# One in four low parts of the weights made by an accumulating DMA instead of a subtraction on VectorE

## The chip, the cores and the metric

The kernel runs on one core of one Trainium2 chip. The metric is device time in microseconds (us) for one call of the whole block. A core has a matrix engine (TensorE, PE in the profile), VectorE (DVE), ScalarE (ACT), GpSimd (POOL) and SyncE (SP), each with an instruction queue of its own, and 16 DMA engines that all queues share.

## The reference

One block of a language model on 256 tokens of width 2048 (T = 256, D = 2048), in float32: a gated feed-forward layer with half its output added, a mixer of an mLSTM and an HGRN2 recurrence behind one wide projection, a cross attention to a memory of 256 rows, and a second feed-forward layer, each behind a root-mean-square norm.

```python
def swiglu(h, w1, w3, w2):
    return (jax.nn.silu(h @ w1) * (h @ w3)) @ w2
...
        h = rmsnorm(x, norm_ffn1[l])
        x = x + 0.5 * swiglu(h, ffn1_w1[l], ffn1_w3[l], ffn1_w2[l])
        h = rmsnorm(x, norm_mix[l])
        (mq, mk, mv, mo, mi, mf, hq, hf, hi, hg, gate_m, gate_h) = jnp.split(h @ w_in[l], split_points, axis=-1)
...
        merged = jax.nn.sigmoid(gate_m) * (y_m @ w_proj_m[l]) + jax.nn.sigmoid(gate_h) * (y_h @ w_proj_h[l])
        x = x + merged @ w_out[l]
        h = rmsnorm(x, norm_xattn[l])
        m = rmsnorm(mem, norm_mem[l])
        x = x + cross_attention(h, m, xattn_wq[l], xattn_wkv[l], xattn_wo[l])
        h = rmsnorm(x, norm_ffn2[l])
        x = x + 0.5 * swiglu(h, ffn2_w1[l], ffn2_w3[l], ffn2_w2[l])
    return rmsnorm(x, norm_final)
```

D_FF is 5632, and w_in has 11272 columns. Nearly all the arithmetic is in products of 256 rows of activations with weights that are each used once.

## The kernel before

**Products in three terms.** TensorE multiplies in the type F32R, which keeps fewer bits than float32. So each operand is held as two tiles: `hi`, the value rounded to F32R, and `lo`, what is left, value minus `hi`. A product is the sum of three matmuls: high by high, high by low, low by high. In `gemm_nat`, whose output has tokens on the partitions, these are lines L200 (activation high, weight `hi`), L201 (activation high, weight `lo`) and L202 (activation low, weight `hi`), in this order, with 512 columns of weight streaming through (344 in three products of the mixer). In `gemm_tr`, whose output is transposed, they are L235, L236 and L237; the weight is the stationary operand there, and `lo` comes third.

**Units and subunits.** The weights of a product are cut into units, of 4 row blocks of 128 by 512 columns in `gemm_nat` and of 8 row blocks by 256 columns in `gemm_tr`: 1 MB each. A unit is loaded by one DMA from SyncE's queue (`load`, L148) into a buffer `wr`, of which there are 4. A unit has two subunits. Each is split by itself into tiles `wh` and `wl` of 128 partitions by 1024 elements, of which there are 4 buffers each: a cast on ScalarE (L159) rounds to `hi`, and a subtraction on VectorE (L160) makes `lo`. The 12 matmuls of a subunit in `gemm_nat`, or 24 of half the columns in `gemm_tr`, then use both.

**The order of the work.** The kernel first writes down a list of steps: subunits, and functions in between (evacuations of a finished product, and work that is put into a background list). `run` walks through the list. Before the matmuls of a subunit are issued, the units of the next 7 subunits are loaded and the next 3 subunits are split; after them `tick` issues what is due by then: transposes of new activations, norms, or one piece of the recurrences. The order in which instructions are issued is the order in each engine's queue. A tile framework adds the waits between engines, so that a cast waits until TensorE has read the last subunit out of the `wh` buffer that it fills, and a load waits until both subunits of the unit in its `wr` buffer are split. These lines set how far ahead all this goes:

```python
    SPLIT_AHEAD = 3
    LOAD_AHEAD = 7
        self.wraw = pool("wraw", 4)
        self.whi = pool("whi", 4)
        self.wlo = pool("wlo", 4)
```

ScalarE also evacuates products (L466 the silu of the feed-forward layers) and rounds activations that were turned (L292, L297, L263); VectorE turns activations in blocks of 32 by 32 (L286), makes their low parts (L293, L298, L264) and adds to the residual (L449, L451). GpSimd does 15 small powers for the norms (`rstd_of`, L407) and two memsets in the mixer; it issues no DMA. ScalarE's queue issues a few DMAs of constants and gains.

Of the kernel before, what the change touches and what calls it, by code (L numbers as in the profile page):

```python
# [12 lines left out]
F32 = mybir.dt.float32  # L13
F32R = mybir.dt.float32r
AF = mybir.ActivationFunctionType
ALU = mybir.AluOpType
# [3 lines left out]
P = 128  # L20
T = 256
# [40 lines left out]
class Sub:  # L62
    def __init__(self, unit, index, mm):
        self.unit, self.index, self.mm = unit, index, mm
        self.hi = self.lo = None
# [8 lines left out]
class Block:  # L74
# [3 lines left out]
    def __init__(self, ctx, tc, a, out):  # L78
        self.tc, self.nc, self.a, self.out = tc, tc.nc, a, out
        pool = lambda name, bufs, **kw: ctx.enter_context(tc.tile_pool(name=name, bufs=bufs, **kw))  # L80
        self.const = pool("const", 1)
        self.xp = pool("xp", 1)
# [3 lines that stand above are left out]
        self.s4 = pool("s4", 22)  # L86
        self.s2 = pool("s2", 4)
        self.small = pool("small", 4)
        self.acc = pool("acc", 4, space=PSUM)
        self.tr = pool("tr", 4, space=PSUM)  # L90
        self.steps = []
        self.now = 0
        self.timed = []
        self.bg = deque()
        self.uid = 0

    def nm(self, s):
        self.uid += 1
        return f"{s}_{self.uid}"
# [14 lines left out]
    def pacc(self, shape, name="pa"):  # L114
        return self.acc.tile(shape, F32, name=self.nm(name), tag="acc")

    # ---- the order of work
    def do(self, fn):
        self.steps.append(fn)

# [29 lines left out]
    def split(self, s):  # L150
        if s.hi is not None:
            return
        u = s.unit
        self.load(u)
        nk = u.nk // u.nsub
        raw = u.raw[:, s.index * nk:(s.index + 1) * nk, :]
        s.hi = self.whi.tile([P, nk, u.n], F32R, name=self.nm("wh"), tag="wh")
        s.lo = self.wlo.tile([P, nk, u.n], F32R, name=self.nm("wl"), tag="wl")
        self.nc.scalar.copy(s.hi, raw)  # L159
        self.nc.vector.tensor_sub(s.lo, raw, s.hi.bitcast(F32))  # L160

    def run(self):
        subs = [s for s in self.steps if isinstance(s, Sub)]
# [11 lines left out]
            i += 1  # L175
        self.flush()

    # ---- products; an operand is a list of (hi, lo) tiles of four 128-row pieces each
    def gemm_nat(self, ops, wap, n0, n, evac, kts=None, row0=0, late=0):
        """late: in the last subunits of the weights the second token tile waits until the first is done."""  # L180
        nc = self.nc
        box = {}
        pairs = ops
        nkt = 4 * len(pairs) if kts is None else kts

        def mm_for(k0, nk):
            def mm(hi, lo, ts=(0, 1)):
                if k0 == 0:
                    box["ps"] = [self.pacc([P, n]) for _ in range(2)]
                if k0 >= nkt - 2 * late and len(ts) == 2:  # L190
                    ts = (0,)
                    box.setdefault("late", []).append(lambda: mm(hi, lo, (1,)))
                for j in range(nk):
                    kt = k0 + j
                    xh, xl = pairs[kt // 4]
                    for t in ts:
                        sl = slice(t * P, (t + 1) * P)
                        a_h, a_l = xh[:, kt % 4, sl], xl[:, kt % 4, sl]
                        o = box["ps"][t]
                        nc.tensor.matmul(o, a_h, hi[:, j, :], start=(kt == 0), stop=False)  # L200
                        nc.tensor.matmul(o, a_h, lo[:, j, :], start=False, stop=False)  # L201
                        nc.tensor.matmul(o, a_l, hi[:, j, :], start=False, stop=(kt == nkt - 1))  # L202
            return mm

        for k0 in range(0, nkt, 4):
            u = Unit(wap, row0 + k0 * P, 4, n0, n, 2)
            for q in range(2):
                self.steps.append(Sub(u, q, mm_for(k0 + 2 * q, 2)))
        if not late:
            self.do(lambda: evac(box["ps"]))  # L210
            return

        def finish():
            evac(box["ps"], (0,))
            for f in box["late"]:
                f()
            evac(box["ps"], (1,))
        self.do(finish)
# [25 lines left out]
        self.do(lambda: evac(box["ps"]))  # L244

    def turn(self, src, gain, dst, halves=(0, 1)):
        """dst: (hi, lo) of the transposed 512 columns that src(t) gives, each times its gain."""
        nc = self.nc
        hi, lo = dst
        for h in halves:  # L250
            ps = self.ps([P, 2, T])
            for j in range(2):
                for t in range(2):
                    c = (2 * h + j) * P
                    nc.tensor.transpose(ps[:, j, t * P:(t + 1) * P], src(t)[:, c:c + P], self.ident)  # L255
            if gain is None:
                nc.scalar.copy(hi[:, 2 * h:2 * h + 2, :], ps)
                nc.vector.tensor_sub(lo[:, 2 * h:2 * h + 2, :], ps, hi[:, 2 * h:2 * h + 2, :].bitcast(F32))
            else:
                for j in range(2):  # L260
                    k = 2 * h + j
                    g = gain[:, k:k + 1]
                    nc.scalar.activation(hi[:, k, :], ps[:, j, :], AF.Copy, scale=g)  # L263
                    nc.vector.scalar_tensor_tensor(  # L264
                        lo[:, k, :], in0=ps[:, j, :], scalar=g, in1=hi[:, k, :].bitcast(F32),
                        op0=ALU.mult, op1=ALU.subtract)
# [6 lines left out]
        self.after(ticks + 1, lambda: self.turn(src, gain, dst, (1,)))  # L273

    def turn_on_vector(self, src, gain, dst, ticks=1):
        """The same for a tile of two token tiles, in blocks of 32 x 32 and without the tensor engine."""
        nc = self.nc
        box = {}
        sv = src.rearrange("p t (k j c) -> p t k j c", k=4, j=4)

        def blocks(i):
            if i == 0:
                box["t"] = self.t4([P, 4, T], name="tt")
            dv = box["t"].rearrange("p k (t i c) -> p t k i c", t=2, i=4)
            for j in range(4):
                nc.vector.transpose(dv[32 * j:32 * j + 32, :, :, i, :], sv[32 * i:32 * i + 32, :, :, j, :])  # L286

        def parts():
            hi, lo = dst
            tt = box["t"]  # L290
            if gain is None:
                nc.scalar.copy(hi, tt)  # L292
                nc.vector.tensor_sub(lo, tt, hi.bitcast(F32))  # L293
                return
            for k in range(4):
                g = gain[:, k:k + 1]
                nc.scalar.activation(hi[:, k, :], tt[:, k, :], AF.Copy, scale=g)  # L297
                nc.vector.scalar_tensor_tensor(lo[:, k, :], in0=tt[:, k, :], scalar=g, in1=hi[:, k, :].bitcast(F32),  # L298
                                               op0=ALU.mult, op1=ALU.subtract)

        for i in range(4):
            self.after(ticks + i, lambda i=i: blocks(i))
        self.after(ticks + 4, parts)

    # ---- pieces
    def setup(self):
        nc, a = self.nc, self.a
        c = self.const.tile([P, C_END], F32, name="cst")
# [177 lines left out]
                self.gemm_nat(LazyOps(lambda us=us: us, f1 - f0), w2, c * 512, 512, evac, row0=f0 * 512,  # L486
                              late=4 if end and last and c == 3 else 0)

    # ---- the two mixers
    def row_scale(self, n):  # L490
        nc = self.nc
        d = self.t2([P, 2, P], name="dg")
# [7 lines left out]
    def mixer(self, norm, chunk_done):  # L500
        nc, a = self.nc, self.a
# [8 lines left out]
        first = [True]  # L510
# [4 lines left out]
                first[0] = False  # L515
            nc.vector.tensor_mul(dst, ps, self.R)

        # forget gates and queries of HGRN2, two heads at a time
        for g in range(4):
            b, hh = g // 2, 2 * (g % 2)  # L520

# [29 lines left out]
            self.gemm_nat(ops, w, 6152 + 512 * j, 512, nat_evac(HB, "g", j, AF.Silu))  # L551
        self.do(lambda: [self.bg.extend(self.hgrn_out(H[b], HB, b)) for b in range(2)])

        # output gate of the mLSTM with its input and forget gates
        MO = [None] * 2

        def evac_o(j):
# [42 lines left out]
            self.gemm_nat(ops, w, 1024 + 512 * j, 512, nat_evac(MV, "v", j))  # L600
        self.do(lambda: self.bg.extend(self.mlstm_out(M, MV, MO)))

        # gates of the merge, projections
        merged = [None] * 4
        G = {}
        for c in range(4):
# [30 lines left out]
            self.gemm_nat(LazyOps(lambda: merged, 4), a["w_out"][0], 512 * c, 512, evac)  # L637

    def hgrn_levels(self, h, b):
        """A^T of four heads. A pair s < t meets at one scale l: both lie in one block of 4 l, in different  # L640
        pieces of l. The decay from s to the end of its piece goes to k, the rest of the decay to q."""
        nc = self.nc
        S = {}
        flat = lambda t: t.rearrange("p h t -> p (h t)")
# [141 lines left out]
        nc.scalar.activation(dst, dst, AF.Silu, bias=self.col["mlstm_conv_b"][:, ch:ch + 1])  # L786

    def mlstm_weights(self, m):
        """exp(log weight - m_t) of every pair and m_t itself, per head, time t on the partitions."""
        nc = self.nc  # L790
        gs = m["gates"]
        m["mt"] = self.small.tile([P, 4, 2], F32, name="mt", tag="mt", bufs=1)
# [42 lines left out]
    def mlstm_scores(self, m):  # L835
# [39 lines left out]
        for h in range(4):  # L875
            ths += [lambda h=h: head(h), lambda h=h: turn(h)]
# [34 lines left out]
            ths += [lambda b=b: turn(b)]  # L911
        return ths

    # ---- cross attention
    def mem_prep(self):
        nc = self.nc
        mem, self.memT = [None] * 4, [None] * 4
# [136 lines left out]
                self.add_to_x(c, ps, 1.0, lambda: chunk_done(c))  # L1054
            self.gemm_nat(LazyOps(lambda: O, 4), wo, 512 * c, 512, evac)

    # ---- all of it
    def build(self):
        nc, a = self.nc, self.a
        N = {}  # L1060
# [24 lines left out]
        def done(name):  # L1085
            return lambda c: self.norm_chunk(begin(name), c)
# [21 lines left out]
        turn_gains = self.setup()  # L1108
        self.ffn(lambda: N["norm_ffn1"], a["ffn1_w1"][0], a["ffn1_w3"][0], a["ffn1_w2"][0], done("norm_mix"))
        self.mixer(lambda: N["norm_mix"], done("norm_xattn"))  # L1110
        # the memory is normalised while the merge is projected
        self.insert_mem()
        self.cross_attention(lambda: N["norm_xattn"], done("norm_ffn2"))

# [6 lines left out]
        n = len(self.steps)  # L1121
# [43 lines left out]
```

## Time and profile before

| | us |
|---|---|
| median of 2 runs | 2570.2 (2569.82 to 2570.57) |
| span of the profiled execution | 2567.6 |
| TensorE busy | 2543.7 |
| VectorE busy | 1649.9 |
| ScalarE busy | 1187.4 |
| GpSimd busy | 14.3 |
| TensorE clock granted, mean | 0.998 |

For the profiled execution only the span from its first to its last instruction is shown, not a time of its own as the runs have; the median stands 2.6 us above that span. The profile comes from this one execution. Busy time counts the time in which an engine has an instruction in work; matmuls are pipelined, so a matmul that is listed with 0.39 us starts 0.23 us after the one before it. HBM reads come to 475.94 MB, 186 GB/s over the span. In an instruction group, the line of the kernel comes first, then engine, operation, what is written and read, the number of instructions, busy time and the mean of one, and the idle time of the engine before them with what ended it.

### The profile page before, as it was taken

The page shows a single profiled execution, that of the slowest core. Times are in us where ns is not written, and L with a number is a line of the kernel's source. Part 1 is how long each engine was busy: PE and PEld are TensorE (multiplying, and loading weights), DVE is VectorE, ACT ScalarE, POOL GpSimd, SP SyncE. Part 2 cuts the span into 40 slices and gives each one's busy share as a digit, 9 for nine tenths or more (in the row PEclk, how much of TensorE's full clock was granted, in tenths as well). Part 3 has the DMA queues.
Part 4 walks back from the last instruction along what each step waited for, and adds up shares of the span by engine and source line. Part 5 has one row for each costly group of instructions (what it writes and reads, how often), then busy time and mean ns, then how long its engine had stood idle before and what let it go on. Part 6 is the DMA issues. An engine that isn't in the chain of part 4 may idle for free.

```text
span 2567.6 us, 31614 instructions
## 1 busy us (share of the span) xinstructions
PE 2543.7 (99%) x12779; PEld 2176.6 (85%) x12779; DVE 1649.9 (64%) x2211; ACT 1187.4 (46%) x1385; POOL 14.3 (1%) x21
## 2 busy tenths in 40 slices
PE   8999999999999999999999999999999999999998
PEld 7888888888899899878888898998888888888887
DVE  5666644757768768576667844556757574456664
ACT  5444434444446555454445544454544443344443
POOL 0000000000000000000000000000000000000000
PEclk9999999999999999999999999999999999999999
DMA  7555555555554435545556555544555555555653
GB/s 266 190 197 197 193 190 192 196 197 187 197 189 166 158 123 191 175 163 193 197 194 215 181 181 197 183 146 158 188 195 195 197 185 197 193 197 186 215 191 130
DMA packets 271987, 480.09 MB, mean 187 GB/s; under 512 B 8008, under 2 KB 71776, under 8 KB 271840
## 3 DMA queue, kind: packets, MB, share of 16 engines
q1 hardware_dynamic: 270688, 476.15, 55.0%
q8 instruction: 100, 1.64, 0.3%
q10 hardware_dynamic: 1152, 1.92, 0.2%
q14 instruction: 47, 0.39, 0.0%
HBM read 475.94 MB, written 2.10 MB: 186 GB/s over the span
## 4 chain that ended last, share of the span: by engine, by line
PE 96%; DVE 2%; issue 1%; DMA 0%; ACT 0%; POOL 0%; SPq 0%; ACTq 0%; POOLq 0%
PE pa L201 27%; PE pa L202 27%; PE pa L200 27%; PE pa L236 4%; PE pa L237 4%; PE pa L235 4%; DVE tt L286 1%; PE ps L718 1%; DVE wl L160 1%; PE ps L255 0%; DMA x<-in_x 0%; PE ps L982 0%; PE ps L981 0%; PE ps L980 0%; POOL rstd L407 0%
## 5 line engine op out<-in xcount | busy, mean ns | idle before, releaser
L160 DVE TENSOR_TENSOR wl<-wr,wh 128x1024 fp32r<-128x1024 f32 (+1 forms) x904 | 1095.6, 1214 | 828.4 <-ACT wh L159 823.0
L159 ACT CAST wh<-wr 128x1024 fp32r<-128x1024 f32 (+1 forms) x904 | 942.2, 1044 | 1163.7 <-PE pa L202 1012.3
L200 PE MATMUL pa<-wh,oh 128*128 128x512 f32 (+1 forms) x3168 | 1233.6, 389 | 2.5 <-ACT wh L159 2.5
L201 PE MATMUL pa<-wl,oh 128*128 128x512 f32 (+1 forms) x3168 | 1228.8, 388 | 6.5 <-DVE wl L160 6.5
L202 PE MATMUL pa<-wh,ol 128*128 128x512 f32 (+1 forms) x3168 | 1228.0, 388 | 0.0
L201 PEld LDWEIGHTS pa<-wl,oh 128*128 128x128 f32 x3168 | 596.2, 188 | 126.8 <-DVE wl L160 8.1
L200 PEld LDWEIGHTS pa<-wh,oh 128*128 128x128 f32 x3168 | 596.0, 188 | 121.6 <-ACT wh L159 2.9
L202 PEld LDWEIGHTS pa<-wh,ol 128*128 128x128 f32 x3168 | 595.9, 188 | 120.3
L235 PE MATMUL pa<-oh,wh 128*128 128x256 f32 x896 | 254.9, 285 | 0.0
L236 PE MATMUL pa<-ol,wh 128*128 128x256 f32 x896 | 253.6, 283 | 0.0
L237 PE MATMUL pa<-oh,wl 128*128 128x256 f32 x896 | 253.6, 283 | 0.0
L236 PEld LDWEIGHTS pa<-ol,wh 128*128 128x128 f32 x896 | 172.0, 192 | 0.1
L235 PEld LDWEIGHTS pa<-oh,wh 128*128 128x128 f32 x896 | 172.0, 192 | 0.1
L237 PEld LDWEIGHTS pa<-oh,wl 128*128 128x128 f32 x896 | 171.9, 192 | 0.0
L286 DVE STREAM_TRANSPOSE tt<-sil 32x256 f32<-32x256 f32 x352 | 153.6, 436 | 6.8
L286 DVE STREAM_TRANSPOSE tt<-x 32x256 f32<-32x256 f32 x144 | 62.8, 436 | 2.7
L297 ACT ACTIVATE oh<-tt,cols 128x256 fp32r<-128x256 f32 x52 | 23.0, 500 | 48.1 <-DVE tt L286 48.1
L292 ACT CAST oh<-tt 128x1024 fp32r<-128x1024 f32 x25 | 26.4, 1055 | 33.2 <-DVE tt L286 33.2
L466 ACT ACTIVATE sil<-pa,rstd 128x512 f32<-128x512 f32 x44 | 29.8, 690 | 18.1 <-PE pa L202 18.0
L263 ACT ACTIVATE oh<-ps,cols 128x256 fp32r<-128x256 f32 x44 | 20.6, 473 | 27.7 <-DVE ol L264 22.8
L471 DVE SCALAR_TENSOR_TENSOR sil<-pa,rstd,sil 128x512 f32<-128x512 f32 x44 | 31.0, 743 | 0.0
L293 DVE TENSOR_TENSOR ol<-tt,oh 128x1024 fp32r<-128x1024 f32 x25 | 30.5, 1219 | 0.2 <-PE pa L201 0.2
(213 smaller groups left out, 734.3 us busy)
## 6 DMA issues: line engine op xcount, KB each, us to landing
wr<-in_ffn_w SPq DMA_DIRECT2D x263, 1024.0 KB, 5.0
wr<-in_w_in SPq DMA_DIRECT2D x80, 1024.0 KB, 5.0
wr<-in_xattn_wkv SPq DMA_DIRECT2D x32, 1024.0 KB, 5.3
wr<-in_w_out SPq DMA_DIRECT2D x16, 1024.0 KB, 5.0
wr<-in_xattn_wq SPq DMA_DIRECT2D x16, 1024.0 KB, 5.4
wr<-in_xattn_wo SPq DMA_DIRECT2D x16, 1024.0 KB, 5.0
wr<-in_w_in SPq DMA_DIRECT2D x12, 688.0 KB, 3.9
wr<-in_w_proj_m SPq DMA_DIRECT2D x8, 1024.0 KB, 5.0
```

The source lines that it names most:

```text
L159: self.nc.scalar.copy(s.hi, raw)
L160: self.nc.vector.tensor_sub(s.lo, raw, s.hi.bitcast(F32))
L200: nc.tensor.matmul(o, a_h, hi[:, j, :], start=(kt == 0), stop=False)
L201: nc.tensor.matmul(o, a_h, lo[:, j, :], start=False, stop=False)
L202: nc.tensor.matmul(o, a_l, hi[:, j, :], start=False, stop=(kt == nkt - 1))
L235: nc.tensor.matmul(o, hi[:, j, sl], xh, start=(kt == 0), stop=False)
L236: nc.tensor.matmul(o, hi[:, j, sl], xl, start=False, stop=False)
L237: nc.tensor.matmul(o, lo[:, j, sl], xh, start=False, stop=(kt == nkt - 1))
L286: nc.vector.transpose(dv[32 * j:32 * j + 32, :, :, i, :], sv[32 * i:32 * i + 32, :, :, j, :])
L293: nc.vector.tensor_sub(lo, tt, hi.bitcast(F32))
L466: nc.scalar.activation(box["s"][:, t, :], ps[t], AF.Silu, scale=norm().rstd[:, t:t + 1])
L471: nc.vector.scalar_tensor_tensor(s[:, t, :], in0=ps[t], scalar=norm().rstd[:, t:t + 1], in1=s[:, t, :], op0=ALU.mult, op1=ALU.mult)
```

## The change

Only `split` changes. A counter numbers the subunits as they are split. From the 9th on, every fourth one makes its `lo` in another way: ScalarE, right behind the cast, writes the negated `hi` into the `wl` tile, and GpSimd's queue issues a DMA that reads the same weights from HBM a second time and adds them onto that tile. The other three subunits keep the subtraction. As a unit has two subunits, the changed one is always the second subunit of every other unit, and its part of `wr` is then read by the cast alone.

```diff
@@ -93,6 +93,7 @@
         self.uid = 0
+        self.nsplit = 0
...
@@ -157,7 +158,14 @@
         s.hi = self.whi.tile([P, nk, u.n], F32R, name=self.nm("wh"), tag="wh")
         s.lo = self.wlo.tile([P, nk, u.n], F32R, name=self.nm("wl"), tag="wl")
         self.nc.scalar.copy(s.hi, raw)
-        self.nc.vector.tensor_sub(s.lo, raw, s.hi.bitcast(F32))
+        self.nsplit += 1
+        if self.nsplit > 8 and self.nsplit % 4 == 0:
+            r0 = u.row0 + s.index * nk * P
+            src = u.wap[r0:r0 + nk * P, u.n0:u.n0 + u.n].rearrange("(k p) n -> p k n", p=P)
+            self.nc.scalar.mul(s.lo, s.hi.bitcast(F32), -1.0)
+            self.nc.gpsimd.dma_start(s.lo, src, accum_op=ALU.add)
+        else:
+            self.nc.vector.tensor_sub(s.lo, raw, s.hi.bitcast(F32))
```

The rest of the diff removes comments.

## The prediction

> **What bounds the kernel now.** I read the engines' busy time first, then the chain of work that ended last, then the groups of the two instructions that make a weight's parts, then the waits.
>
> ```profile
> PE 2543.7 (99%) x12779; PEld 2176.6 (85%) x12779; DVE 1649.9 (64%) x2211; ACT 1187.4 (46%) x1385; POOL 14.3 (1%) x21
> PE 96%; DVE 2%; issue 1%; DMA 0%; ACT 0%; POOL 0%; SPq 0%; ACTq 0%; POOLq 0%
> L160 DVE TENSOR_TENSOR wl<-wr,wh 128x1024 fp32r<-128x1024 f32 (+1 forms) x904 | 1095.6, 1214 | 828.4 <-ACT wh L159 823.0
> L159 ACT CAST wh<-wr 128x1024 fp32r<-128x1024 f32 (+1 forms) x904 | 942.2, 1044 | 1163.7 <-PE pa L202 1012.3
> ```
>
> TensorE is busy for 2543.7 of 2567.6 us and carries 96% of the chain. The subtraction that the change partly removes is VectorE's largest group, 904 times 1.214 us, but VectorE stands idle for a third of the span, and 823.0 us of its idle time is spent waiting for the cast. The chain of the subtraction is: TensorE frees a buffer, ScalarE casts, VectorE subtracts. What matters is whether TensorE ever waits for its end:
>
> ```profile
> ACT wh L159 <- PE pa L202: 1012.3, 629, 3.8
> PE pa L201 <- DVE wl L160: 6.5, 4, 2.7
> PEld pa L201 <- DVE wl L160: 8.1, 6, 3.1
> SPq L148 <- DVE wl L160: 2082.1, 405, 10.6
> ```
>
> The cast waits for TensorE, so the split runs as far ahead as its buffers allow. TensorE waits for a low part 4 times, 6.5 us in all. That is nearly all that a faster VectorE could give, and the whole gap between TensorE's busy time and the span is 23.9 us, under 1%. The last line says that the SyncE queue's weight loads start when a subtraction has freed their buffer.
>
> **How much time a low part has.** This is the timeline of a steady stretch; each row is start, length, engine, line.
>
> ```profile
> 301.20 0.39 PE L200 MATMUL pa<-wh,oh 128*128 128x512 f32 x1
> 301.40 1.05 ACT L159 CAST wh<-wr 128x1024 fp32r<-128x1024 f32 x1 [1.67 <-PE pa L202]
> 302.49 1.23 DVE L160 TENSOR_TENSOR wl<-wr,wh 128x1024 fp32r<-128x1024 f32 x1 [1.50 <-ACT wh L159]
> 303.93 0.39 PE L200 MATMUL pa<-wh,oh 128*128 128x512 f32 x1
> 306.64 0.39 PE L200 MATMUL pa<-wh,oh 128*128 128x512 f32 x1
> 309.37 0.39 PE L200 MATMUL pa<-wh,oh 128*128 128x512 f32 x1
> 309.59 0.39 PE L201 MATMUL pa<-wl,oh 128*128 128x512 f32 x1
> ```
>
> A subunit of weights is 12 matmuls, and begins at 301.20, 303.93, 306.64, 309.37: one per 2.72 us. The cast that starts at 301.40 fills the buffer that the subunit before 301.20 has left; with four buffers and a split three ahead it is used in the subunit that starts at 309.37, and its low part in the second matmul, at 309.59. The subtraction has it ready at 302.49 + 1.23 = 303.72, 5.87 us early.
>
> **Part by part.** The page counts 904 subunits. From the 12th on every fourth is changed: (904 - 8) / 4 = 224. They divide by form:
>
> ```profile
> L160 DVE TENSOR_TENSOR wl<-wr,wh 128x1024 fp32r<-128x1024 f32 x880 | 1074.9, 1223 | 821.8 <-ACT wh L159 816.6
> L160 DVE TENSOR_TENSOR wl<-wr,wh 128x688 fp32r<-128x688 f32 x24 | 20.7, 872 | 6.6 <-ACT wh L159 6.4
> L235 PE MATMUL pa<-oh,wh 128*128 128x256 f32 x896 | 254.9, 285 | 0.0
> L685 ACT ACTIVATE kt<-suf 128x1024 f32<-128x1024 f32 x6 | 6.3, 1057 | 0.0
> L292 ACT CAST oh<-tt 128x1024 fp32r<-128x1024 f32 x25 | 26.4, 1055 | 33.2 <-DVE tt L286 33.2
> L466 ACT ACTIVATE sil<-pa,rstd 128x512 f32<-128x512 f32 x44 | 29.8, 690 | 18.1 <-PE pa L202 18.0
> ```
>
> The transposed products take 8 of the L235 matmuls per subunit, so 112 subunits, of which 28 are changed. Of the 24 narrow ones 6 are, which leaves 190 wide ones.
>
> *VectorE* loses 224 x 1.22 us = 273 us. It is off the chain; the gain is at most the 6.5 us above, and I take 6.5.
>
> *ScalarE* gains 224 negations of 128x1024. No such instruction is in the trace; the nearest row is L685, the same size, 1.057 us, so 237 us. The cast and the negation fill 2.11 of 2.72 us. What is queued behind the negation is the evacuation of a finished product (two L466, 1.38 us) or a turned operand (one L292, 1.06 us); such a subunit overruns by 0.5 to 0.8 us and the next cast is late by that. Before an ordinary low part the 5.87 us cover it. Before a changed one nothing does: about a quarter of the 22 pairs and 25 casts, 12 x 0.8 = 9 us.
>
> *GpSimd* gains 224 DMA issues, each waiting for its negation. Queued behind them are the rstd powers, 15 in all, which come at the end of a subunit when the negation (done 2.1 us into it) is past; I take nothing, at worst 12 x 2.1 = 25 us; no gain is possible, for an instruction put behind another cannot start earlier.
>
> *The DMA* is the term that decides. The weights' second reading is 218 x 0.524 + 6 x 0.352 = 116 MB more. What a transfer costs here:
>
> ```profile
> q1 hardware_dynamic: 270688, 476.15, 55.0%
> wr<-in_ffn_w SPq DMA_DIRECT2D x263, 1024.0 KB, 5.0
> gf<-in_norm_final ACTq DMA_DIRECT2D x2, 512.0 KB, 3.6
> mem<-in_mem SPq DMA_DIRECT2D x4, 512.0 KB, 7.0
> ```
>
> ```profile
> 301.02 0.37 SPq L148 DMA_DIRECT2D wr<-in_ffn_w  x1
> 301.50:302.00 0.50, 0.50 (x4) 0.42 (x3) 0.00 (x0) 0.50 (x1) 0.00 (x0) 1.00 0.00 0
> 302.00:302.50 0.50, 0.50 (x4) 0.42 (x3) 0.01 (x1) 0.46 (x1) 0.00 (x0) 1.00 0.66 90
> 303.50:304.00 0.50, 0.50 (x4) 0.42 (x3) 0.22 (x1) 0.00 (x0) 0.00 (x0) 1.00 1.07 418
> 305.00:305.50 0.50, 0.50 (x3) 0.40 (x3) 0.29 (x1) 0.18 (x1) 0.00 (x0) 1.00 0.69 262
> 305.50:306.00 0.50, 0.50 (x4) 0.41 (x3) 0.50 (x1) 0.00 (x0) 0.00 (x0) 1.00 0.00 0
> ```
>
> The last two columns of the half-microsecond stretches are the share of the DMA engines and GB/s. A 1 MB load issued at 301.02 moves data from 302.00 (0.98 us later) to 305.50, at full share in between, and lands after 5.0 us, 0.5 us behind its last data. So 1 MB takes 3.5 us of all engines, and 512 KB half, 1.75 us.
>
> Now put the change into this stretch. The cast ends at 302.45, the negation at 302.45 + 1.06 = 303.51, and GpSimd may issue: 309.59 - 303.51 = 6.08 us remain until TensorE needs the tile. But the changed subunit is always the second of its unit, and its buffer is now read last by the cast and not by the subtraction. So the next load is issued at about 302.48 and its data starts at 303.46, just ahead of the accumulation. Both use the same engines, so whichever goes first, the pair is done at 303.46 + 3.5 + d, where d is the time that the accumulation keeps the engines, provided that GpSimd's issue brings the first data before 306.96; the tile lands 0.5 us later. The break-even is d = 309.59 - 0.5 - 306.96 = 2.13 us.
>
> No accumulation is in the trace. A plain 512 KB gives d = 1.75 as the lower end. It cannot be less, as the same bytes are fetched. As the upper end I take four times this, 7.0, worked out as a read, a second read of the tile, and as much again for the addition. I choose d = 3.5, the price of the 1 MB row, because the engines have to fetch two operands for each element stored. Then the tile lands at 303.46 + 3.5 + 3.5 + 0.5 = 310.96, 1.37 us late.
>
> The Trainium skill's page "Collectives: The Full Stack", section "The bandwidth ceiling", has a reduction at half the rate of a copy, because the adding DMA reads two sources through one ring; nothing run here shows it, and by it the sum is the one taken.
>
> In the transposed products a subunit is longer, as two casts show:
>
> ```profile
> 1482.44 1.05 ACT L159 CAST wh<-wr 128x1024 fp32r<-128x1024 f32 x1 [1.53 <-PE pa L236]
> 1485.32 1.05 ACT L159 CAST wh<-wr 128x1024 fp32r<-128x1024 f32 x1 [1.83 <-PE pa L236]
> ```
>
> 2.88 us instead of 2.72 gives 3 x 0.16 = 0.48 us more, so 0.89 us late. A late tile stops TensorE once in four subunits; the three others are split meanwhile, and the next accumulation starts only when TensorE has moved on, so waits add up one for one. The narrow six count like the wide ones: fewer bytes, but shorter subunits.
>
> Sum: 196 x 1.37 + 28 x 0.89 = 269 + 25 = 294 us; ScalarE 9; VectorE -6.5. 2567.6 + 296.5 = 2864 us of span. The runs' median, 2570.2, lies 2.6 us over the profiled span, which I take as what lies around it: 2867 us.
>
> **The rivals.** *The accumulation hides (25%).* If the engines hold it for less than 2.13 us, it lands in time: at d = 1.75 at 309.21, 0.38 us early, and the time is 2567.6 + 9 - 6.5 + 2.6 = 2573, down to about 2561 if the displaced casts are covered and VectorE's relief also removes waits inside the mixers. For it: 512 KB on ScalarE's queue landed in 3.6 us beside the loads, and 6.08 are there; the engines are idle for almost half of the span (55.0%). Against it: 512 KB behind the loads on their own queue took 7.0, and this transfer always meets a load.
>
> The Trainium skill's page "DMA: Bandwidth & Descriptors", section "Anatomy of one DMA", speaks for this rival: about 2.0 us and the bytes at 436 GB/s for one DMA from GpSimd, 3.2 us for 512 KB, an estimate for a plain one. By it the tile is there 2.9 us early; the row nearest to it, 3.6 us on ScalarE's queue, is close to it, but neither adds.
>
> *The accumulation is dearer than two reads (30%).* At d = 7.0, or if GpSimd needs over 3.4 us to bring the first data, the tile is 4.87 us late: 196 x 4.87 + 28 x 4.39 = 1077 us, 3650 us in all. For it: the DMA writes a 4-byte type other than its source's and reads back the tile, small pieces of 2 KB; GpSimd does nothing of this kind in the trace, so its issue is unpriced. Against it: the capacity isn't short at d = 3.5 (two loads and one accumulation, 10.5 us, in 10.9 + 1.4), so it needs a slow adder. I give 17% to 3050 to 3400 and 13% to beyond.
>
> *Faster by over 2% (1%).* VectorE's relief would have to remove 51 us, and TensorE waits 23.9 us in all, head and tail included.
>
> **How the numbers follow.** The forecast has 44%, and its own range is 2625 to 3050: tiles late by 0.24 to 2.1 us, d from 2.4 to 4.3. A measurement of this kernel can tell about 2%, 51 us, from no change. Slower by more: 44 + 30 = 74%; no difference 25%; faster 1%. The range starts at 2558, which takes in the hidden case, and ends at 3400, where a tile is 3.7 us late on average and d is 5.8; 13% lie above and about 2% below.
>
> **What would show it.** In the changed profile, waits of TensorE's L201 and L237 line for the wl tile from a DMA, about 224 of them and 294 us, instead of 4; a GpSimd queue with 116 MB whose time to landing is about 7.5 us; SyncE's loads issued after the cast. TensorE's busy share falls to 89%, at an unchanged clock. If the landing is under 6 us and the waits are absent, d was too large; if the landing is over 9 us, the adder or GpSimd's issue is what I underpriced. It would also be wrong if TensorE waits at other tiles than those, for then something queued behind the negation or the issue is what is late.

## The result, and the profile after

The changed kernel takes 2852.47 us (median of 2852.14 and 2852.79) against 2570.2 before: a ratio of 1.1099, 95% interval 1.1066 to 1.1131. It is 282 us slower; 2867 was predicted. These lines of the page of the changed kernel answer to those of before. The cast is now L160, the negation L165, the accumulating DMA L166, the subtraction L168, and TensorE's three terms are L208, L209 (the one that reads `wl`) and L210.

```profile
PE 2619.8 (92%) x12779; PEld 2177.9 (76%) x12779; DVE 1394.2 (49%) x1987; ACT 1420.5 (50%) x1611; POOL 287.0 (10%) x245
q1 hardware_dynamic: 270688, 476.15, 51.3%
q0 software_dynamic: 68096, 116.42, 24.1%
DMA 44%; PE 31%; ACT 15%; issue 5%; DVE 5%; POOL 0%; ACTq 0%; SPq 0%; POOLq 0%; DVEq 0%
L209 PE MATMUL pa<-wl,oh 128*128 128x512 f32 (+1 forms) x3168 | 1256.4, 397 | 200.5 <-DMA wl<-in_ffn_w 126.8
wl<-in_ffn_w POOLq DMA_DIRECT2D x130, 512.0 KB, 6.5
```

VectorE is freed of 256 us, and nothing comes of it. The chain that ended last, 96% TensorE before, is now 44% DMA, and TensorE's L209 sits idle for 200.5 us waiting for a DMA that writes `wl`. The new queue q0 brings 116.42 MB and holds the 16 engines for 24.1% of 2850.3 us, which is 3.07 us for each of the 224 accumulations of 0.52 MB. The loads of q1 hold them for 3.07 us per MB (51.3% of 2850.3 us over 476.15 MB). Byte for byte an accumulation costs 1.9 times a load.

The waits of the changed kernel, in total, number and longest (PEld is TensorE's load of the stationary operand, SPq SyncE's queue):

```profile
PEld pa L209 <- DMA wl<-in_ffn_w: 181.5, 130, 4.9
PE pa L209 <- DMA wl<-in_ffn_w: 126.8, 129, 4.5
PE pa L209 <- DMA wl<-in_w_in: 39.5, 26, 4.8
PE pa L245 <- DMA wl<-in_w_in: 8.1, 5, 2.4
SPq L149 <- ACT wh L160: 550.0, 202, 7.2
```

Of the 130 changed tiles of the feed-forward layers 129 are listed as holding up a matmul, and all 130 the load of its operand. Over all weights the waits of matmuls for these DMAs come to 212.8 us in 195 waits. SyncE's loads now also wait for the cast, as foreseen. One changed tile in the timeline:

```profile
331.40 1.05 ACT L160 CAST wh<-wr 128x1024 fp32r<-128x1024 f32 x1 [2.68 <-PE pa L210]
332.47 0.37 SPq L149 DMA_DIRECT2D wr<-in_ffn_w  x1
332.48 1.06 ACT L165 ACTIVATE wl<-wh 128x1024 fp32r<-128x1024 f32 x1
333.84 1.20 POOL L166 DMA_DIRECT2D wl<-in_ffn_w  x1 [10.62 <-ACT wl L165]
339.30 0.39 PE L208 MATMUL pa<-wh,oh 128*128 128x512 f32 x1
340.27 0.50 PE L209 MATMUL pa<-wl,oh 128*128 128x512 f32 x1 [0.58 <-DMA wl<-in_ffn_w]
```

The cast frees the weight buffer, and the next load is issued at 332.47, before the negation has even begun. GpSimd picks up 0.30 us after the negation's end (333.54) and issues for 1.20 us. L209 should start at 339.53 and starts at 340.27, 0.74 us late. What the DMA engines do meanwhile (each row has the stretch, its length, the busy time of the five engines, and last the granted clock, the share of the DMA engines and GB/s):

```profile
334.40:336.90 2.50, 2.50 (x13) 2.07 (x12) 1.22 (x1) 0.83 (x2) 0.64 (x1) 1.00 1.04 387
336.90:339.40 2.50, 2.50 (x13) 1.98 (x11) 1.22 (x1) 0.94 (x1) 0.00 (x0) 1.00 1.09 199
339.40:339.90 0.50, 0.29 (x2) 0.00 (x0) 0.00 (x0) 0.40 (x1) 0.00 (x0) 1.00 0.33 53
```

The shares of the two queues in the two long stretches, one after the other:

```profile
q1 hardware_dynamic: 472, 0.95, 100.1%
q0 software_dynamic: 238, 0.49, 107.8%
```

For 2.5 us the engines work for the load's queue, at 387 GB/s; then for 2.5 us for the accumulation's, at 199 GB/s with the engines just as busy; then it is 0.87 us until TensorE goes on.

### The profile page after: what moved, and what is told of

Same layout as the page of the kernel before. It is cut to its first block, busy times and chain, and to the rows that moved or that the text cites. A ratio compares the mean times of both kernels' runs of the same rounds, so it can differ in the third digit from the quotient of the medians.

```text
span 2850.3 us, 32183 instructions
## 1 busy us (share of the span) xinstructions
PE 2619.8 (92%) x12779; PEld 2177.9 (76%) x12779; DVE 1394.2 (49%) x1987; ACT 1420.5 (50%) x1611; POOL 287.0 (10%) x245
## 3 DMA queue, kind: packets, MB, share of 16 engines
q1 hardware_dynamic: 270688, 476.15, 51.3%
q0 software_dynamic: 68096, 116.42, 24.1%
## 4 chain that ended last, share of the span: by engine, by line
DMA 44%; PE 31%; ACT 15%; issue 5%; DVE 5%; POOL 0%; ACTq 0%; SPq 0%; POOLq 0%; DVEq 0%
DMA wl<-in_ffn_w 29%; PE pa L209 9%; PE pa L210 7%; ACT wl L165 6%; DMA wl<-in_w_in 6%; ACT wh L160 6%; PE pa L208 6%; DMA wl<-in_xattn_wkv 4%; PE pa L245 2%; DVE tt L294 2%; PE pa L244 2%; PE pa L243 2%; DMA wl<-in_w_out 1%; DMA wl<-in_xattn_wo 1%; DVE wl L168 1%
## 5 line engine op out<-in xcount | busy, mean ns | idle before, releaser
L160 ACT CAST wh<-wr 128x1024 fp32r<-128x1024 f32 (+1 forms) x904 | 941.3, 1042 | 1182.3 <-PE pa L210 1067.6
L209 PE MATMUL pa<-wl,oh 128*128 128x512 f32 (+1 forms) x3168 | 1256.4, 397 | 200.5 <-DMA wl<-in_ffn_w 126.8
L168 DVE TENSOR_TENSOR wl<-wr,wh 128x1024 fp32r<-128x1024 f32 (+1 forms) x680 | 826.2, 1215 | 1247.1 <-ACT wh L160 1243.3
L208 PE MATMUL pa<-wh,oh 128*128 128x512 f32 (+1 forms) x3168 | 1238.9, 391 | 2.4 <-ACT wh L160 2.4
L210 PE MATMUL pa<-wh,ol 128*128 128x512 f32 (+1 forms) x3168 | 1235.8, 390 | 0.0
L209 PEld LDWEIGHTS pa<-wl,oh 128*128 128x128 f32 x3168 | 599.4, 189 | 392.4 <-DMA wl<-in_ffn_w 181.5
L208 PEld LDWEIGHTS pa<-wh,oh 128*128 128x128 f32 x3168 | 599.5, 189 | 125.4 <-ACT wh L160 2.8
L210 PEld LDWEIGHTS pa<-wh,ol 128*128 128x128 f32 x3168 | 599.8, 189 | 116.1
L166 POOL DMA_DIRECT2D wl<-in_ffn_w x130 | 156.7, 1205 | 1421.3 <-ACT wl L165 1333.8
L165 ACT ACTIVATE wl<-wh 128x1024 fp32r<-128x1024 f32 (+1 forms) x224 | 235.6, 1052 | 5.7
L166 POOL DMA_DIRECT2D wl<-in_w_in x46 | 57.0, 1239 | 495.0 <-ACT wl L165 484.1
```

The source lines that it names most:

```text
L165: self.nc.scalar.mul(s.lo, s.hi.bitcast(F32), -1.0)
L166: self.nc.gpsimd.dma_start(s.lo, src, accum_op=ALU.add)
```

## The experiments

Each is an edit of the changed kernel unless said otherwise. Two theories stood at first. By the shared-engines theory, the prediction's, the tile is late because the load and an accumulation at half rate use the same engines one after the other. By the rival, a GpSimd DMA has a fixed latency that no other transfer touches.

**A plain copy in place of the addition.**

```diff
-            self.nc.gpsimd.dma_start(s.lo, src, accum_op=ALU.add)
+            self.nc.gpsimd.dma_start(s.lo, src)
```

> Edit: the DMA of every fourth low part is a plain copy of the weight onto the tile, without the addition; GpSimd's issue, the waits and the bytes from HBM stay (the low part is wrong then, so one in four is the whole weight and not what is left of it). Shared-engines theory (the accumulation holds the DMA engines for two reads, 2.5 to 3.5 us, behind a 1 MB load): the copy holds them for 1.25 to 1.75 us less, so a tile that lands 8.85 us after its cast began, 0.7 to 0.8 us too late, comes in time; 2573 to 2620 us, the queue's share of the engines falls from 24% to about 12 or 13%, time to landing to 5.0 to 5.3 us. Fixed-latency theory (issue on GpSimd and a fixed time to landing, whatever is moved): 2852 us, landing 6.5 us as before.

Measured: 2641.25 us, 1.028 (1.0264 to 1.0295). Page of the run:

```profile
q0 software_dynamic: 68096, 116.42, 15.4%
L166 POOL DMA_DIRECT2D wl<-in_ffn_w x130 | 92.9, 715 | 1354.0 <-ACT wl L165 1319.8
wl<-in_ffn_w POOLq DMA_DIRECT2D x130, 512.0 KB, 5.3
```

The same bytes, copied, hold the engines for 15.4% of 2639.3 us / 224 = 1.81 us instead of 3.07, and land 1.2 us sooner. The edit also shortens GpSimd's issue, 0.72 us instead of 1.20, so not all of this need be data. The rival's fixed latency, by which nothing would have changed, is refuted. The share is above the 12 or 13% expected, and the time is 21 us above the upper end, with some tiles still late.

**Negation first, cast second.**

```diff
-        self.nc.scalar.copy(s.hi, raw)
...
-            self.nc.scalar.mul(s.lo, s.hi.bitcast(F32), -1.0)
+            self.nc.scalar.mul(s.lo, raw, -1.0)
             self.nc.gpsimd.dma_start(s.lo, src, accum_op=ALU.add)
+            self.nc.scalar.copy(s.hi, raw)
         else:
+            self.nc.scalar.copy(s.hi, raw)
```

> Edit: in a changed subunit ScalarE makes the negated high part first, straight from the loaded weight, and the cast after it; GpSimd can issue 1.06 us earlier and the next load, which the cast now frees, comes 1.06 us later. Fixed-latency theory: every tile lands 1.06 us earlier, 224 x 1.06 = 237 us, about 2615 us. Shared-engines theory: the pair of load and accumulation ends when the engines have moved both; with the load starting 1.06 us later the pair ends later and only the order of the two can help, so the tile gains between -0.3 and 1.06 us: 2615 to 2900 us, most likely a gain of half of 1.06, 2735 us.

Measured: 2994.64 us, 1.1664 (1.1644 to 1.1683), outside both expectations: with the accumulation issued a microsecond earlier, and the load a microsecond later, the kernel is 142 us slower than the changed one. Timeline and stretches of this run (negation L164, cast L166, DMA L165):

```profile
335.39 1.06 ACT L164 ACTIVATE wl<-wr 128x1024 fp32r<-128x1024 f32 x1 [1.32 <-PE pa L210]
336.75 1.20 POOL L165 DMA_DIRECT2D wl<-in_ffn_w  x1 [11.96 <-ACT wl L164]
337.41 0.37 SPq L149 DMA_DIRECT2D wr<-in_ffn_w  x1
346.09 0.50 PE L210 MATMUL pa<-wl,oh 128*128 128x512 f32 x1 [2.12 <-DMA wl<-in_ffn_w]
```

```profile
341.50:345.50 4.00, 2.47 (x11) 1.69 (x10) 1.87 (x2) 1.71 (x2) 0.00 (x0) 1.00 1.09 255
q0 software_dynamic: 245, 0.47, 65.3%
q1 hardware_dynamic: 278, 0.54, 43.0%
```

The load, freed only by the second ScalarE instruction, now comes after GpSimd's issue instead of before it. It no longer gets out of the way: the last two rows are the shares of the queues from 341.5 to 345.5, where both run together at 255 GB/s. The tile is used 10.7 us after ScalarE began (335.39 to 346.09) instead of 8.87 (331.40 to 340.27), and the median landing is 8.9 us. Counted from the issue of the load, the landing moves less: 8.9 - 0.66 = 8.2 us here, 6.5 + 1.37 = 7.9 us in the changed kernel. So most of the loss is the later start of the load, 0.95 us later after ScalarE began (337.41 - 335.39 against 332.47 - 331.40): the tile lands only when both are through. The rival would have had each tile 1.06 us earlier.

**Half the load.** Both subunits are split from the first half of the unit, and the second half is not loaded.

```diff
-            src = u.wap[u.row0:u.row0 + u.nk * P, u.n0:u.n0 + u.n].rearrange("(k p) n -> p k n", p=P)
...
+            h = u.nk // 2
...
+            src = u.wap[u.row0:u.row0 + h * P, u.n0:u.n0 + u.n].rearrange("(k p) n -> p k n", p=P)
...
-        raw = u.raw[:, s.index * nk:(s.index + 1) * nk, :]
+        raw = u.raw
```

> Edit: each weight load brings only the first half of its unit (512 KB), and both subunits are split from it, so the second subunit multiplies with the first one's weights; the accumulations, their issue and their bytes stay. Shared-engines theory: the load that an accumulation meets is 1.25 to 1.75 us shorter, the tile lands that much earlier and the waits go but for a few: 2573 to 2620 us. Fixed-latency theory: 2852 us.

Measured: 2765.28 us, 1.0766 (1.0748 to 1.0784). This is where the prediction's picture fell short: with half the load gone, 195 of the 282 us stay, and the landing goes from 6.5 to 6.0 us only. Stretches of this run, with GpSimd's issue at 339.37:

```profile
339.37 1.20 POOL L167 DMA_DIRECT2D wl<-in_ffn_w  x1 [10.06 <-ACT wl L166]
```

```profile
340.00:340.50 0.50, 0.50 (x4) 0.42 (x3) 0.00 (x0) 0.50 (x1) 0.50 (x1) 1.00 0.96 365
341.50:342.00 0.50, 0.50 (x4) 0.42 (x3) 0.41 (x1) 0.00 (x0) 0.00 (x0) 1.00 0.85 66
342.50:343.00 0.50, 0.50 (x4) 0.41 (x3) 0.00 (x0) 0.50 (x1) 0.00 (x0) 1.00 0.96 160
343.50:344.00 0.50, 0.50 (x4) 0.42 (x3) 0.50 (x1) 0.00 (x0) 0.00 (x0) 1.00 1.13 209
```

The short load (365 GB/s at 340.0) is over at 341.0. The engines are then busy at 66 GB/s, and reach the accumulation's 200 GB/s only between 3.1 and 4.1 us after the issue began (160 GB/s from 342.5, 209 from 343.5). What holds the data back until then no run shows. So there are two chains: the accumulation's own (about 3 us from issue to full rate, then its data) and the pair's (the load to its end, then the accumulation's data). In the changed kernel the pair's is the longer, 6.5 us against the 6.0 that are left here. Shortening the load alone leaves the other chain.

**Half the accumulated bytes.** In the first form VectorE subtracts the other half:

```diff
...
+            a, b = slice(0, nk // 2), slice(nk // 2, nk)
+            self.nc.scalar.mul(s.lo[:, a, :], s.hi[:, a, :].bitcast(F32), -1.0)
+            self.nc.gpsimd.dma_start(s.lo[:, a, :], src, accum_op=ALU.add)
+            self.nc.vector.tensor_sub(s.lo[:, b, :], raw[:, b, :], s.hi[:, b, :].bitcast(F32))
```

> Edit: only the first row block of a changed low part is negated and accumulated (256 KB), the second is subtracted on VectorE; the negation is half as long. Own-chain theory (the accumulation's own chain, pick-up and issue on GpSimd, ramp, data at half rate and landing, is longer than the 6.08 us a tile has, and the load beside it adds little): the fixed part of the 6.5 us landing stays, about 4 us, the data part halves, landing 5.0 to 5.3 us, issue 0.5 us earlier, so nearly all tiles come in time: 2573 to 2610 us. Shared-engines theory (load and accumulation end together): the pair ends 1.25 to 1.75 us earlier, landing 4.8 to 5.2 us from an issue 0.5 us earlier, 2573 to 2590 us. If the time to landing hardly depends on the bytes (6.0 us or more): 2700 us and above.

Measured: 2733.47 us, 1.0637 (1.062 to 1.0653), landing 6.4 us. Taken alone this says that bytes hardly matter. But VectorE's half subtraction reads the weight buffer, and so the next load was issued 0.20 us before GpSimd's issue instead of 1.37 us (332.47 to 333.84) in the changed kernel:

```profile
336.51 0.37 SPq L149 DMA_DIRECT2D wr<-in_ffn_w  x1
336.71 0.87 POOL L167 DMA_DIRECT2D wl<-in_ffn_w  x1 [10.55 <-DVE wl L168]
```

The second row puts GpSimd's wait down to VectorE's half subtraction, which ended at 336.48; the negation ended at 336.42, so either can have released it. The load's place is over half of the way to that in the run with the negation first. The second form leaves the other half as the negated high part and keeps the load where it was:

```diff
-            src = u.wap[r0:r0 + nk * P, u.n0:u.n0 + u.n].rearrange("(k p) n -> p k n", p=P)
+            src = u.wap[r0:r0 + nk * P // 2, u.n0:u.n0 + u.n].rearrange("(k p) n -> p k n", p=P)
...
-            self.nc.gpsimd.dma_start(s.lo, src, accum_op=ALU.add)
+            self.nc.gpsimd.dma_start(s.lo[:, :nk // 2, :], src, accum_op=ALU.add)
```

> Edit: as the changed kernel, negation and timing of the loads included, but the DMA adds only the first row block of a changed low part (256 KB); the second keeps the negated high part alone and is wrong. This is the half-size run without its side effect (there the next load was freed 1 us later, by VectorE). Two-chains theory (a tile is late by the longer of two chains: its own, about 3.0 us from GpSimd's issue to full rate and 2.5 us of data, and the pair's, 2.5 us of the load and then 2.5 us of the accumulation; each then 0.85 us to land): both are 1.25 us shorter, landing 5.1 to 5.3 us, 2580 to 2630 us. If the time to landing hardly depends on the bytes, as the 6.4 us of the half-size run could be read: 2730 us or more.

Measured: 2632.78 us, 1.0237 (1.022 to 1.0254); landing 5.1 us. Half the bytes are worth 220 us of the 282. The first form is 101 us slower (2733 against 2633), with the load's issue 1.2 us closer to the accumulation's; its shorter negation, by which GpSimd issues 0.4 us sooner after the cast, does not make up for it. Then both halved:

```diff
...
-        raw = u.raw[:, s.index * nk:(s.index + 1) * nk, :]
+        raw = u.raw
...
-            self.nc.gpsimd.dma_start(s.lo, src, accum_op=ALU.add)
+            self.nc.gpsimd.dma_start(s.lo[:, :nk // 2, :], src, accum_op=ALU.add)
```

> Edit: half the bytes accumulated and half the bytes loaded (both subunits split from the first half of the unit). Two-chains theory: with the load halved alone (2765 us) the own chain was left, and it is 1.25 us shorter here; landing 4.7 to 5.0 us, 2573 to 2600 us, a little under the run with half the accumulated bytes alone. If load and accumulation only share the engines in proportion: the same bytes in total as one load, also 2573 to 2600 us. If a fixed landing of 6 us is what counts: 2765 us.

Measured: 2589.12 us, 1.0076 (1.006 to 1.0091). The landings on the pages of the three runs (half load, half accumulation, both):

```profile
wl<-in_ffn_w POOLq DMA_DIRECT2D x130, 512.0 KB, 6.0
```

```profile
wl<-in_ffn_w POOLq DMA_DIRECT2D x130, 256.0 KB, 5.1
```

```profile
wl<-in_ffn_w POOLq DMA_DIRECT2D x130, 256.0 KB, 4.3
```

With the load halved, half the bytes take the landing from 6.0 to 4.3 us. Both chains have to be shorter for the wait to go, as the two-chains theory says.

**More time for the tile.** The split four subunits ahead:

```diff
-    SPLIT_AHEAD = 3
-    LOAD_AHEAD = 7
+    SPLIT_AHEAD = 4
+    LOAD_AHEAD = 5
...
-        self.wraw = pool("wraw", 4)
...
+        self.wraw = pool("wraw", 3)
+        self.whi = pool("whi", 5)
+        self.wlo = pool("wlo", 5)
```

> Edit: the changed kernel with the split four subunits ahead instead of three, five buffers of high and low parts, and for their room three weight buffers instead of four with loads five subunits ahead. A tile has one subunit, 2.72 us, more. Shared-engines theory: landing stays at 6.5 us, 8.8 us are there, and the waits go: 2565 to 2590 us. Fixed-latency theory: the same, as the time that a tile has is what counts for it too. If instead something that is queued behind the negation or the issue were what holds TensorE, most of the loss would stay, over 2700 us.

Measured: 2582.02 us, 1.0048 (1.0033 to 1.0063). The same 224 accumulations, landing 6.7 us after their issue, cost 12 us when 8.8 us are there for them; L209 waits for three tiles of the feed-forward layers instead of 129:

```profile
PE pa L209 <- DMA wl<-in_w_in: 10.1, 3, 3.8
PE pa L209 <- DMA wl<-in_ffn_w: 4.0, 3, 2.1
```

The same edit in the kernel before:

```diff
-    SPLIT_AHEAD = 3
-    LOAD_AHEAD = 7
+    SPLIT_AHEAD = 4
+    LOAD_AHEAD = 5
...
+        self.wraw = pool("wraw", 3)
+        self.whi = pool("whi", 5)
+        self.wlo = pool("wlo", 5)
```

> Edit: the kernel before (all low parts by subtraction) with the buffers and look-ahead of the run with four subunits ahead: what is left between that run (2582 us) and this is the price of the accumulations when nobody waits for them. If deeper splitting itself costs nothing: 2566 to 2574 us, and the accumulations cost about 12 us. If the three weight buffers are what costs: 2582 us, and the accumulations cost nothing.

Measured: 2567.0 us, 0.9988 (0.998 to 0.9997). The deeper split costs nothing by itself. It is the fastest version here, without any accumulation; the accumulations cost 15 us in it, so VectorE's relief gains nothing even where hardly anything waits for them.

**ScalarE's part alone.** The negation of every fourth subunit stays, the accumulation goes, and VectorE subtracts everywhere, which overwrites the negation; against the changed kernel:

```diff
-            self.nc.gpsimd.dma_start(s.lo, src, accum_op=ALU.add)
-        else:
-            self.nc.vector.tensor_sub(s.lo, raw, s.hi.bitcast(F32))
+        self.nc.vector.tensor_sub(s.lo, raw, s.hi.bitcast(F32))
```

> Edit: the kernel before, and on every fourth subunit ScalarE also writes the negated high part into the tile, which VectorE's subtraction then overwrites; no accumulation, the result is the right one. This prices the ScalarE term alone. Prediction's term: 9 us, about 2579 us. If the negation is covered everywhere: 2570 us. If what is queued behind ScalarE matters more: over 2590 us.

Measured: 2573.88 us, 1.0014 (1.0006 to 1.0023): 4 us, between nothing and the 9 of the prediction's term. A tile still has its subtraction's early end here, so what the negation costs where a tile is already late no run shows.

**One in eight.**

```diff
-        if self.nsplit > 8 and self.nsplit % 4 == 0:
+        if self.nsplit > 8 and self.nsplit % 8 == 0:
```

> Edit: one low part in eight is accumulated, 112 instead of 224, each as in the changed kernel. If each changed tile costs by itself: 1.26 us each, 112 x 1.26 = 141, about 2711 us. If tiles hold up one another, or the stretches of half clock come from their density: 2640 to 2690 us. If the cost were capacity of the DMA engines, it would vanish: 2575 us.

Measured: 2771.66 us, 1.0785 (1.0771 to 1.08), 202 us for 112 tiles: 1.80 us each, more than in any expectation. The same with the fourth of eight:

```diff
-        if self.nsplit > 8 and self.nsplit % 4 == 0:
+        if self.nsplit > 8 and self.nsplit % 8 == 4:
```

> Edit: one low part in eight as in the run at 2772 us, but the fourth of each eight subunits and not the eighth. In that run ScalarE's queue holds the rounding of a turned operand (which itself waits for VectorE) between the cast and the negation of 25 of 112 tiles; here of none. If that, the place, is why a tile cost 1.80 us there and 1.26 us in the changed kernel: 1.1 to 1.3 us each here, 2695 to 2715 us. If it is the lower density of changed tiles (TensorE runs undisturbed longer in between, loads are closer): 2760 to 2780 us.

Measured: 2722.17 us, 1.0599 (1.058 to 1.0617), 152 us or 1.36 each. So it is the place more than the density. The mean granted clocks are 0.984 and 0.992 in these two runs and 0.991 in the changed kernel, against 0.998 before. The share of the clock that is missing, times the span, comes to about 39, 17 and 21 us more than before. Without it a tile costs 1.45, 1.21 and 1.17 us. ScalarE in the run with the eighth:

```profile
71.69 1.05 ACT L160 CAST wh<-wr 128x1024 fp32r<-128x1024 f32 x1 [1.62 <-PE pa L210]
74.85 1.05 ACT L300 CAST oh<-tt 128x1024 fp32r<-128x1024 f32 x1 [2.10 <-DVE tt L294]
75.80 1.06 ACT L165 ACTIVATE wl<-wh 128x1024 fp32r<-128x1024 f32 x1
```

Here the rounding of a turned operand stands in ScalarE's queue between the cast and the negation and itself waits 2.10 us for VectorE, so the negation comes 3.06 us after the cast's end. The queue has this order for 25 of that run's tiles, for none of the fourth-place run's and for none of the changed kernel's. That it accounts for the whole difference is not shown.

**One in two, with the deeper split.** The buffers of the run with four subunits ahead, and

```diff
-        if self.nsplit > 8 and self.nsplit % 4 == 0:
+        if self.nsplit > 8 and self.nsplit % 2 == 0:
```

> Edit: the run with four subunits ahead (2582 us), but one low part in two accumulated (448 instead of 224). With the waits out of the way this asks for the capacity of the DMA engines. An accumulation held them for 3.07 us in the changed kernel (24.1% of 2850 us, 224 times) and a load for 3.07 us too; one of each in every two subunits is 6.1 us where TensorE needs 5.44. If the engines are the limit then: 452 x 6.1 = 2760 us or more. If the accumulation's latency is all that ever counts and the deeper split hides it: 2580 to 2600 us.

Measured: 2662.29 us, 1.0357 (1.034 to 1.0374).

```profile
q0 software_dynamic: 136192, 232.85, 51.9%
q1 hardware_dynamic: 270688, 476.15, 50.7%
wl<-in_ffn_w POOLq DMA_DIRECT2D x260, 512.0 KB, 8.6
PE pa L209 <- DMA wl<-in_ffn_w: 37.4, 47, 3.1
```

The shares of the two queues add up to 102.6%, the landing takes 8.6 us of the 8.8 that are there, and TensorE waits again. This fits the capacity of the engines as the limit; that nothing else adds to it was not tested. The price was as expected: 102.6% of 2660.2 us is 6.0 us for each of 452 pairs (6.1 expected). The expected time was too long because the share can pass 100%, as in the stretches above (1.04 to 1.13).

## Why the prediction was right

*TensorE is the bound and VectorE's relief is worth nothing:* right. VectorE's busy time fell by 256 us and nothing was gained, not even with the deeper split.

*The wait is at L209 for the DMA, about 224 times:* right; 195 waits of TensorE are listed. Of the loss of 282 us, the listed waits are 213. A wait is listed from the modelled end of the matmul before it, which lies 0.16 us behind the start that was due (339.69 against 339.53), 31 us for 195 waits. The clock is 21. That locates 264 us; 18 are not located. The transposed products' share of the listed waits is 12 us (25 forecast), small as the extra 0.48 us said. Of the other signs, TensorE's busy share fell to 92% (89 forecast), and the clock did not stay as it was (0.991 against 0.998).

*The accumulation reads two operands, so 512 KB keeps the engines for 3.5 us:* over-sized; 3.07 us of all engines by the queue's share, 2.5 us at 199 GB/s in the stretch shown. The ratio of two to a copy was right (1.9 byte for byte against the loads); the price of the 1 MB load that was taken for it was too high. That load's 3.5 us run from its first data to its last, with a share of 0.66 in the first half microsecond; by its queue's share (55.0% of 2567.6 us over 476.15 MB, 1.05 MB a load) it held all engines for 3.1 us. The Trainium skill's page "Collectives: The Full Stack", section "The bandwidth ceiling", puts a reduction between cores at half the rate of a copy, because the add needs two source reads; the trace agrees on the rate, 199 against 387 GB/s, and no run shows the second read itself. The page "DMA: Bandwidth & Descriptors" of the Trainium skill, section "Anatomy of one DMA", gives an estimate of 3.2 us for a plain 512 KB from GpSimd; here it landed in 5.3 us beside the loads, and the measurement decides.

*Load and accumulation end together, whichever goes first:* this is what the changed kernel does. The load's data runs from about 333.45, 0.98 us after its issue, to 336.90: 3.45 us, 3.5 forecast. Then come 2.5 us of accumulation (3.5 forecast) and 0.87 us to TensorE's start (0.5 forecast), so the tile shown is 0.74 us late and not 1.37, and the median landing is 6.5 us and not 7.5. With these terms the prediction's sum is 0.98 + 3.45 + 2.5 + 0.87 = 7.8 us from the load's issue. An estimate by it, with the data's time halved where the bytes are halved or only copied, against the medians of the other runs (tiles of the feed-forward layers, all in us):

| run | load issued, from GpSimd's issue | sum, from GpSimd's issue | measured landing |
|---|---|---|---|
| half accumulated, load where it was | -1.36 | 5.2 | 5.1 |
| half accumulated, VectorE the other half | -0.20 | 6.4 | 6.4 |
| plain copy | -1.36 | 5.2 | 5.3 |
| negation first | +0.66 | 8.5 | 8.9 |
| half load | -1.36 | 4.7 | 6.0 |
| both halved | -1.36 | 3.5 | 4.3 |

Where the whole load is there, the sum holds within 0.1 us, and within 0.5 where the load comes second and both run together. It fails where the load is short. There the accumulation's own chain is what counts, which the prediction had only as a proviso ("GpSimd's issue brings the first data before 306.96"): 0.30 us of pick-up, 1.20 us of issue, and full rate only 3.1 to 4.1 us after the issue began. So the half load gave 87 us where the expectation had over 230.

That 282 us were measured and 297 forecast is in part luck. A tile is less late in the middle than forecast, 0.74 us in the one shown, and the spread of the landings (waits of up to 4.5 us) and the clock bring the mean to 1.26 us per tile. The prediction had neither. A changed subunit that is the first of its unit, whose cast frees no load, was not run; it would show the load's part without a change of bytes.

*ScalarE 9 us:* mis-sized; 4 us by itself, where no tile waits for an accumulation. *VectorE -6.5 us:* TensorE's waits for VectorE's low parts are gone from the list, but their worth cannot be told from the rest. *GpSimd's queue, nothing:* not tested by itself.

*The rivals.* The hidden case is real but needs another kernel: with 2.72 us more per tile the loss is 12 us. The break-even was placed right, in that half the bytes (d near 1.3) nearly reach it and the whole does not. The dear adder did not appear.

## What to carry to other kernels

An accumulating DMA replaces a vector instruction only if the tile can wait for it: count pick-up, the time until the data runs at full rate, data at half rate and landing (here 0.3 + 3.1 + 2.5 + 0.9 = 6.8 us for 512 KB beside a load, against the subtraction's 1.2) against the look-ahead, and buy look-ahead first. When a buffer's last reader changes, look at which transfer is freed and when: the tile is ready when the load that it meets and the accumulation are both done, and where the load was issued later the kernel was 101 and 142 us slower. And do not move work off an engine that the chain of waits does not show.

## What was not expected of the hardware

After some waits TensorE runs at half clock for a while. Stretches of the changed kernel around a wait of 2.1 us:

```profile
351.00:352.00 1.00, 0.45 (x2) 0.03 (x1) 0.00 (x0) 0.74 (x1) 0.00 (x0) 1.00 0.54 88
352.00:353.00 1.00, 0.00 (x0) 0.00 (x0) 0.66 (x1) 0.31 (x1) 0.00 (x0) 1.00 0.75 209
353.00:354.00 1.00, 0.47 (x2) 0.43 (x3) 0.56 (x1) 0.00 (x0) 0.00 (x0) 1.00 1.04 395
354.00:355.00 1.00, 1.00 (x5) 0.77 (x4) 0.00 (x0) 0.00 (x0) 0.00 (x0) 0.62 0.94 360
355.00:356.00 1.00, 1.00 (x4) 0.80 (x3) 0.00 (x0) 0.00 (x0) 0.00 (x0) 0.50 0.21 80
356.00:357.00 1.00, 1.00 (x4) 0.73 (x3) 0.00 (x0) 0.00 (x0) 0.00 (x0) 0.50 0.00 0
357.00:358.00 1.00, 1.00 (x5) 0.81 (x4) 0.00 (x0) 0.01 (x1) 0.00 (x0) 0.67 0.00 0
```

TensorE is idle from 351.45 to 353.53, and then the granted clock is 0.50 for 0.76 + 1 + 1 + 0.66 = 3.4 us, which loses 1.7 us more. The Trainium skill's page "TensorE: Matmul & The Clock Gate", section "Part 1", has the clock set by a free-running window of 4096 cycles, about 3.4 us; the length agrees with this row. Few waits are followed by it: the clock's 21 us of the changed kernel are about 12 such stretches at 1.7 us, for 195 waits of about 1.1 us. Longer waits bring more of them, but not one each. The run with the negation first has 109 waits of about 1.9 us in the feed-forward layers, as this row of its waits says, in total and number:

```profile
PE pa L210 <- DMA wl<-in_ffn_w: 206.0, 109, 3.5
```

It has a mean clock of 0.974, about 73 us of its 2990.7 more than is missing before, or some 43 stretches for its 165 listed waits for accumulations. What decides which wait is followed by one stays open.
